# Output projection of the first pass in float16 pairs, both halves' weights resident, and the mLSTM half of blocks 3 to 8 behind the first attention

## The chip, the cores and the metric

The kernel runs on one core of a Trainium2 chip. The time is the device time of one execution in microseconds (us), as the median of several runs. TensorE multiplies matrices, VectorE and ScalarE work on vectors and on functions of them, GpSimd is a third, slower vector engine, and SyncE issues DMAs. In the profile they are PE (with PEld for weight loads), DVE, ACT, POOL and SP. Each engine takes its instructions in a fixed order that is laid down when the kernel is built.

## What is computed

One layer of a hybrid backbone: attention and an mLSTM side by side on one input projection, one output projection for both, then a SwiGLU feed-forward. There are 128 prompt tokens and 1024 latent tokens, so nine blocks of 128 tokens.

```python
D_MODEL = 1024; N_Q_HEADS = 8; HEAD_DIM = 64; MLSTM_HEADS = 4; D_FF = 2816

def trunk_layer(x, mods, ..., w_out, norm2_w, w_gu, w_down, rope, ctx_kv, init_f, init_b):
    h = rmsnorm(x, norm1_w) * (1 + sc1) + sh1
    aq, ak, av, mq, mk, mv, mo, mg = jnp.split(h @ w_in, SPLIT_POINTS, axis=-1)
    ...                                            # rmsnorm and axial rotary on aq, ak
    attn_o = attention(aq, keys, vals)             # latent tokens see 128 cached + 1024 keys
    hm, st_f, st_b = mlstm_bidir(...)              # both directions, chunks of 128
    hm = rmsnorm(hm, mlstm_norm_w) * jax.nn.sigmoid(mo)
    mix = jnp.concatenate([attn_o, hm], axis=-1) @ w_out      # (tokens, 1024) @ (1024, 1024)
    x = x + g1 * mix
    h2 = rmsnorm(x, norm2_w) * (1 + sc2) + sh2
    x = x + g2 * swiglu(h2, w_gu, w_down)
```

## The kernel before

**Passes.** The nine blocks are worked in three passes of three blocks (CB = 3) through attention, output projection, norm2 and feed-forward. Pass 0 has the prompt (block 0) and latent blocks 1 and 2, pass 1 blocks 3 to 5, pass 2 blocks 6 to 8. Before pass 0 come the input projections, the mLSTM scan of all blocks (its result goes to `hm_d` in device memory) and the first query projections.

**Number formats.** A float32 product is made of three products of a high and a low part. The input projection uses float16 pairs with a power-of-two scale (lines 487 to 489). The output projection and the feed-forward use pairs in a rounded float32 (`F32R`, in the profile f32 or fp32r): a weight block of 128x1024 is loaded as `raw`, ScalarE casts it to `whi` (line 151), and VectorE or GpSimd subtracts to get `wlo` (line 134).

**Attention** (`attention`). Blocks 1 and 2 have eight heads each; I number the 16 heads 0 to 15. A head is six score matmuls into `S` (line 1075), the row maximum on VectorE (1077), the exponential on ScalarE (1078), two small VectorE steps, the scaled high half `ph` on ScalarE (1081), the low half `pl` on VectorE (1082), and two DMA transposes (1083, 1084). `S` has one buffer. Two heads later the values product `po` follows (18 matmuls, line 999), then `ol` on ScalarE and `oT` on VectorE (1001, 1003). The next query blocks (`QREST`, in three groups) are projected beside the first heads by `weave`, 24 steps of projection to 9 of attention; their rotary runs on GpSimd (lines 639 to 657) with tables in the pool `qp`.

**Output projection of pass 0.** `w_out` has two halves of 512 rows: the attention's and the mLSTM's. `prefill` makes the mLSTM half of all nine blocks beside the attention: per block a row of `hm_d` is loaded and transposed (line 113) into `aTh`/`aTl`, then 24 matmuls of 512 columns (`out_block`, lines 1184 to 1186) are added to x, for blocks 0 to 5 in the resident `x1`, for blocks 6 to 8 through buffers `t2` (a ring of three): load x (1233), product (1235), sum on GpSimd (1236), store to `x1_d` (1237). `attn_out` then makes the attention half of blocks 0 to 2 as their heads finish, and norm2 of each: `stats` (a square on ScalarE, `rsqrt` with some ten small VectorE steps), `y` on ScalarE (1297), eight transposes, `fl`, `aTh` and `aTl`. Behind it `gate_up_pair` makes the gate/up products of the first two blocks of 128 columns of the feed-forward for 256 of the 384 tokens, and the main feed-forward starts with the other 128 tokens of them.

**What sets the order.** The generators yield pieces, and loops such as `weave` draw from several of them; the engines' orders come out of that and of a list scheduler with priorities (`hot`). The first attention draws one piece of `prefill` and `attn_out` for each of its own; behind it, the next attention is drawn 0.3 to 1 while the rest of `attn_out` runs. Buffers from pools are reused, so a tile of a new pool waits for the last user of the memory below it.

## Time and profile before

| | |
|---|---|
| median of 3 runs | 1619.37 us (1618.15 to 1621.2) |
| profiled execution | 1617.88 us, its span 1616.1 us |
| TensorE busy | 1521.3 us, 94% |
| VectorE, ScalarE, GpSimd busy | 940.1, 730.2, 615.8 us |
| mean granted TensorE clock | 0.968 |
| instructions | 23209 |

How to read it: a span is the time between the first and the last instruction. A row of instructions reads: start, duration, engine, line of the kernel, operation, output <- inputs, shape, count, and in brackets the idle time of the engine ahead of it with what ended it. A row of a group has count, busy time and mean duration, then idle time with its releasers. A matmul's duration overlaps that of its neighbours. The granted clock is a share of full speed.

### The profile page before, as it was taken

Reading aid. Unit: us, or ns where it says so; the run is one execution under the profiler, and the core shown is the slowest. Engines: PE = TensorE matmul, PEld = TensorE weight load, DVE = VectorE, ACT = ScalarE, POOL = GpSimd, SP = SyncE. Lnnn points to the kernel's source line nnn. Section 1 sums busy time; section 2 is a strip of 40 time slices with the busy share of each in tenths; the row PEclk is TensorE's granted clock in tenths of the full one; section 3 lists DMA queues with packets and bytes.
Section 4 is the critical chain, followed back from the end, with each engine's and each line's share of the span. In section 5 each row is a group of like instructions: output and inputs, shape, how many; then the busy total and the mean of one; then the engine's idle time right before and its main releaser. Section 6 shows DMA issues by size and latency. Waiting matters only on the chain. (4 is left out here: it accounts for less than half of the span.)

```text
span 1616.1 us, 23209 instructions
## 1 busy us (share of the span) xinstructions
PE 1521.3 (94%) x8688; PEld 1260.8 (78%) x8688; DVE 940.1 (58%) x1821; ACT 730.2 (45%) x1240; POOL 615.8 (38%) x376
## 2 busy tenths in 40 slices
PE   5899999899788868999999999999999999999996
PEld 2655665576557758988999999898898989999995
DVE  3944353947787565677753547767764474332445
ACT  3744343435454455655532344565552443333322
POOL 0411020503247453433345344443344445544443
PEclk8899999999899987999999999999999999999998
DMA  9445353211165664787843546787774445534441
GB/s 344 132 131 144 102 134 73 84 19 32 41 171 119 147 159 100 166 194 169 190 146 118 156 144 208 189 180 165 169 178 124 142 134 174 156 122 147 143 130 66
DMA packets 383270, 227.98 MB, mean 141 GB/s; under 512 B 169174, under 2 KB 345766, under 8 KB 383158
## 3 DMA queue, kind: packets, MB, share of 16 engines
q1 hardware_dynamic: 382598, 225.68, 52.9%
q8 instruction: 68, 1.11, 0.3%
q10 hardware_dynamic: 560, 0.83, 0.1%
q14 instruction: 44, 0.36, 0.1%
HBM read 178.80 MB, written 9.33 MB: 116 GB/s over the span
## 5 line engine op out<-in xcount | busy, mean ns | idle before, releaser
L134 POOL TENSOR_TENSOR wlo<-raw,whi 128x1024 fp32r<-128x1024 f32 x146 | 357.8, 2454 | 450.3 <-ACT whi L151 416.4
L151 ACT CAST whi<-raw 128x1024 fp32r<-128x1024 f32 x219 | 224.3, 1025 | 372.0 <-DMA raw<-in_w_gu_dram 127.8
L1334 PE MATMUL mm<-aTl,whi 128*128 128x384 f32 (+2 forms) x1088 | 366.8, 337 | 0.0
L1335 PE MATMUL mm<-aTh,wlo 128*128 128x384 f32 (+2 forms) x1088 | 366.4, 337 | 0.0
L1333 PE MATMUL mm<-aTh,whi 128*128 128x384 f32 (+2 forms) x1088 | 365.1, 337 | 0.9 <-DVE tn L1361 0.9
L1333 PEld LDWEIGHTS mm<-aTh,whi 128*128 128x128 f32 x1088 | 206.9, 190 | 2.1 <-DVE tn L1361 1.5
L1334 PEld LDWEIGHTS mm<-aTl,whi 128*128 128x128 f32 x1088 | 206.9, 190 | 1.0 <-POOL aTl L134 0.3
L1335 PEld LDWEIGHTS mm<-aTh,wlo 128*128 128x128 f32 x1088 | 207.0, 190 | 0.1
L134 DVE TENSOR_TENSOR wlo<-raw,whi 128x1024 fp32r<-128x1024 f32 (+1 forms) x73 | 88.2, 1208 | 132.9 <-ACT whi L151 132.7
L1152 PE MATMUL mm<-whi,hl 128*128 128x512 f32 x372 | 147.0, 398 | 1.0 <-ACT hl L1365 0.9
L1153 PE MATMUL mm<-wlo,hl 128*128 128x512 f32 x372 | 147.2, 397 | 0.0
L1154 PE MATMUL mm<-whi,hl 128*128 128x512 f32 x372 | 144.4, 397 | 0.7 <-POOL hl L134 0.7
L1082 DVE SCALAR_TENSOR_TENSOR pl<-pr,st,ph 128x1152 f16<-128x1152 f32 x64 | 109.5, 1711 | 46.7 <-ACT ph L1081 46.6
L487 PE MATMUL wi<-ipair,hT 128*128 128x384 f16 (+2 forms) x384 | 124.9, 326 | 2.8 <-ACT ipair L215 2.8
L488 PE MATMUL wi<-ipair,hT 128*128 128x384 f16 (+2 forms) x384 | 124.9, 325 | 0.0
L489 PE MATMUL wi<-ipair,hT 128*128 128x384 f16 (+2 forms) x384 | 124.4, 325 | 0.3 <-POOL hT L134 0.3
L1361 DVE SCALAR_TENSOR_TENSOR tn<-tn,mm 128x384 f32<-128x384 f32 (+2 forms) x68 | 36.7, 540 | 144.4 <-PE mm L1335 110.0
L134 POOL TENSOR_TENSOR hl<-tn,hl 128x384 fp32r<-128x384 f32 x66 | 81.9, 1241 | 96.5 <-ACT hl L1365 90.4
L1142 DVE TENSOR_TENSOR x<-x,t 128x512 f32<-128x512 f32 x102 | 116.1, 1158 | 0.8
L1078 ACT ACTIVATE pr<-S,st 128x1152 f32<-128x1152 f32 x64 | 78.3, 1223 | 80.4 <-DVE st L1077 77.6
L1141 DVE TENSOR_TENSOR t<-mm,gl 128x512 f32<-128x512 f32 x106 | 70.8, 683 | 40.6 <-PE mm L1154 15.8
L1077 DVE TENSOR_REDUCE st<-S 128x1 f32<-128x1152 f32 x64 | 86.5, 1351 | 13.2 <-PE S L1075 12.8
(370 smaller groups left out, 2678.0 us busy)
## 6 DMA issues: line engine op xcount, KB each, us to landing
raw<-in_w_gu_dram SPq DMA_DIRECT2D x132, 512.0 KB
raw<-in_w_down_dram SPq DMA_DIRECT2D x60, 512.0 KB
a<-in_w_ada_dram SPq DMA_DIRECT2D x32, 512.0 KB
gl<-g_d SPq DMA_DIRECT2D x36, 256.0 KB
aw<-in_w_ada_dram SPq DMA_DIRECT2D x16, 512.0 KB
iraw<-in_w_in_dram SPq DMA_DIRECT2D x32, 256.0 KB
raw<-in_w_out_dram SPq DMA_DIRECT2D x15, 512.0 KB
x<-in_x_sample_dram SPq DMA_DIRECT2D x13, 512.0 KB
```

Of the source, the lines that this page charges most:

```text
L134: (dve if eng == "dve" else pool).tensor_tensor(out=out, in0=full, in1=hi, op=ALU.subtract)
L151: nc.scalar.copy(hi[:, :n], raw[:, :n])
L487: mm(ps[:, :n], ah, wh[:, k % 2, c0 : c0 + n], start=(k == 0), stop=False)
L488: mm(ps[:, :n], ah, wl[:, k % 2, c0 : c0 + n], start=False, stop=False)
L489: mm(ps[:, :n], al, wh[:, k % 2, c0 : c0 + n], start=False, stop=(k == KD - 1))
L1142: eng.tensor_tensor(out=x1[:, cs], in0=x1[:, cs], in1=t, op=ALU.add)
L1152: mm(ps, ah, wh[:, k % 2, :], start=(k == 0), stop=False)
L1153: mm(ps, ah, wl[:, k % 2, :], start=False, stop=False)
L1154: mm(ps, al, wh[:, k % 2, :], start=False, stop=(k == nk - 1))
L1333: mm(ps, wh[:, k, :], th[:, k, :], start=(k == 0), stop=False)
L1334: mm(ps, wh[:, k, :], tl[:, k, :], start=False, stop=False)
L1335: mm(ps, wl[:, k, :], th[:, k, :], start=False, stop=(k == KD - 1))
```

## The change

`out_scale` reads all of `w_out` once, early, for one power-of-two scale; the mLSTM half's four blocks stay resident. `out_pairs` makes float16 pairs of them: `hpair` in the pool `xp`, whose memory lies over that of `qp`, and `apair` for the attention half, which is loaded a second time. The left-hand sides become float16 pairs too (`halves16`), and the products are scaled back as they are added (`add_scaled`). `prefill` is now one generator for each block, and `attn_first` takes the place of `attn_out` in pass 0. `first_rows` sets the order: blocks 0 and 1 of the mLSTM half, then attention block 0, then one more mLSTM block, attention block 1, and the other mLSTM blocks behind the first attention, beside attention block 2. The next attention is no longer drawn in this part. The scaling of v goes from VectorE to ScalarE; `weave` is 24 to 10.

ScalarE around heads 8 and 9 (`pr` is the exponential, `ph` the high half, `S` the scores). Before:

```order
L1078 ACTIVATE pr_5416,st_5419<-S_5420,st_5419 128x1152
L1001 ACTIVATE ol_5499<-po_5480,vsc 64x256
L1081 ACTIVATE ph_5417<-pr_5416,st_5419 128x1152
L1220 CAST aTh_5254<-mm_5875 128x4x128
L151 CAST xhi<-xraw 128x1024
L1078 ACTIVATE pr_5451,st_5454<-S_5455,st_5454 128x1152
L1081 ACTIVATE ph_5452<-pr_5451,st_5454 128x1152
```

After, from head 8's exponential to head 9's second step, with the four weight pairs between them:

```order
L1127 ACTIVATE pr_5479,st_5482<-S_5483,st_5482 128x1152
L1130 ACTIVATE ph_5480<-pr_5479,st_5482 128x1152
L974 ACTIVATE hpair_5308<-oraw_4452,osc 128x1024
L978 CAST hpair_5311<-oraw_4454 128x1024
L974 ACTIVATE hpair_5315<-oraw_4456,osc 128x1024
L978 CAST hpair_5318<-oraw_4458 128x1024
L1127 ACTIVATE pr_5514,st_5517<-S_5518,st_5517 128x1152
L1050 ACTIVATE ol_5555<-po_5536 64x256
L1243 ACTIVATE lhs_5458<-mm_5451,hms 128x512
L1240 CAST lhs_5533<-oT_4879 128x512
L1130 ACTIVATE ph_5515<-pr_5514,st_5517 128x1152
```

The pairs were `whi` casts ahead of head 4 before; now they stand between two heads. TensorE, before, at head 3, where the projection matmuls of the mLSTM half stand around its scores:

```order
L1186 MATMUL mm_5349<-whi_5269,aTl_5255 128x512
L1075 MATMUL S_5018<-kst_4226,qT_4739 128x384 x6
L999 LDWEIGHTS vs
L999 MATMUL po_4956<-phT_4766,vs 128x256
L999 LDWEIGHTS vs
L999 MATMUL po_4956<-plT_4767,vs 128x256
L1184 MATMUL mm_5349<-whi_5275,aTh_5254 128x512
L1184 MATMUL mm_5398<-whi_5257,aTh_5254 128x512
```

After, at heads 5 to 7 (the three `S` rows), where only values stand between scores:

```order
L1048 MATMUL po_5232<-plT_5024,vs 128x256
L1124 MATMUL S_5205<-kst_4235,qT_4793 128x384 x6
L1124 MATMUL S_5350<-kst_4235,qT_4793 128x384 x6
L1048 LDWEIGHTS vs
L1048 MATMUL po_5411<-phT_5168,vs 128x256
L1124 MATMUL S_5380<-kst_4235,qT_4793 128x384 x6
L1048 LDWEIGHTS vs
L1048 MATMUL po_5411<-plT_5169,vs 128x256
```

The first projection matmul of the change stands behind head 9's scores. ScalarE after, at head 11 (its exponential is the last row but one here; `jk` to `fl` are norm2 of block 0):

```order
L1330 ACTIVATE jk_5613,s_1107_5612<-x_1040_5294 128x1024
L1346 ACTIVATE y_5634<-x_1040_5294,ry_5616 128x512
L1346 ACTIVATE y_5666<-x_1040_5294,ry_5616 128x512
L1354 ACTIVATE fl_5633<-mm_5636,shift_76,scale_75 128x128 x3
L1127 ACTIVATE pr_5647,st_5650<-S_5651,st_5650 128x1152
L1354 ACTIVATE fl_5633<-mm_5668,shift_76,scale_75 128x128 x3
```

Norm2 of block 0 moved from behind the attention to the middle of it. TensorE after, at the end of the first attention: the last values (18 matmuls, the last of them here) and the first matmuls of mLSTM block 3 (`lhs_5987`) and attention block 2 (`lhs_5976`):

```order
L1048 MATMUL po_5953<-plT_5829,vs 128x256
L1232 LDWEIGHTS lhs_5987
L1232 MATMUL mm_5990<-hpair_5308,lhs_5987 128x512
L1233 LDWEIGHTS lhs_5987
L1233 MATMUL mm_5990<-hpair_5308,lhs_5987 128x512
L1232 LDWEIGHTS lhs_5976
L1232 MATMUL mm_6006<-apair_5330,lhs_5976 128x512
```

Blocks 3 to 8 of the mLSTM half stand behind the last values now, where the scores of the next attention were. The diff, cut to its core:

```diff
+    def out_load(half):
+        raws = []
+        for n in range(2):
+            for j in range(2):
+                r0 = half * 512 + 2 * j * P
+                raw = wp.tile([P, 1024], F32, name=nm("oraw"), tag="wlo", bufs=5)
+                dma(raw..., w_out[r0 : r0 + 2 * P, n * 512 : (n + 1) * 512]...)
+                raws.append(raw)
+        return raws
+
+    def out_scale(kept):
+        for half in range(2):
+            raws = out_load(half)
+            for _ in range(4):
+                yield
+            for j, raw in enumerate(raws):
+                jk = wp.tile([P, 1024], BF16, name=nm("jk"), tag="raw", bufs=2)
+                act(jk, raw, AF.Abs, accum_out=osc[:, 4 * half + j : 4 * half + j + 1])
+                yield
+        kept.extend(raws)
+        dve.tensor_reduce(out=osc[:, 8:9], in_=osc[:, 0:8], axis=AX.X, op=ALU.max)
+        yield from power_scale(gp, one1, osc[:, 8:9], osc[:, 9:11])
...
+    def out_pairs(raws, new):
+        ws = [[], []]
+        for j, raw in enumerate(raws):
+            w = new(j)
+            hi, lo = w[:, 0], w[:, 1]
+            if j % 2 == 0:
+                act(hi, raw, AF.Copy, scale=osc[:, 9:10])
+                dve.scalar_tensor_tensor(out=lo, in0=raw, scalar=osc[:, 9:10], in1=hi, op0=ALU.mult, op1=ALU.subtract)
+            else:
+                act(raw, raw, AF.Copy, scale=osc[:, 9:10])
+                nc.scalar.copy(hi, raw)
+                sub(lo, raw, hi, "pool")
+            ws[j // 2].append(...)
+        return ws
...
-    weave(linear_tok(w_q, 0, 512, ev_q, QFIRST), beside((scan, 3.0), (key_stacks(), 0.2)), 16, 16)
+    weave(linear_tok(w_q, 0, 512, ev_q, QFIRST), beside((scan, 3.0), (key_stacks(), 0.2), (oscale, 1.2)), 16, 16)
...
-        dve.tensor_scalar(out=v, in0=v, scalar1=vsc[:, 0:1], scalar2=None, op0=ALU.mult)
-        dve.tensor_copy(vs[:, i0 : i0 + 5, :, 0], v)
+        act(v, v, AF.Copy, scale=vsc[:, 0:1])
+        nc.scalar.copy(vs[:, i0 : i0 + 5, :, 0], v)
...
-    weave(linear_tok(w_q, 0, 512, ev_q, QREST, bank), att, 24, 9)
+    weave(linear_tok(w_q, 0, 512, ev_q, QREST, bank), att, 24, 10)
...
+    def halves16(src, scale):
+        t = wp.tile([P, 2, 4, P], F16, name=nm("lhs"), tag="wlo", bufs=5)
+        if scale is None:
+            nc.scalar.copy(t[:, 0], src)
+            sub(t[:, 1], src, t[:, 0], "dve")
+        else:
+            act(t[:, 0], src, AF.Copy, scale=scale)
+            dve.scalar_tensor_tensor(out=t[:, 1], in0=src, scalar=scale, in1=t[:, 0], op0=ALU.mult, op1=ALU.subtract)
+        return t[:, 0], t[:, 1]
+
+    def add_scaled(x, ps, inv, g):
+        t = t2()
+        dve.scalar_tensor_tensor(out=t, in0=ps, scalar=inv, in1=g, op0=ALU.mult, op1=ALU.mult)
+        pool.tensor_tensor(out=x, in0=x, in1=t, op=ALU.add)
...
+    def attn_first(i, a, o, ws, gs, gx, ahead=None):
+        x1 = a["x1"][i]
+        with hot(500):
+            th, tl = halves16(o, None)
+        yield
+        for n in range(2):
+            cs = slice(n * 512, (n + 1) * 512)
+            ps = out_block(ws, n, th, tl)
+            with hot(200):
+                add_scaled(x1[:, cs], ps, osc[:, 12:13], gx[n] if i == 0 else gs[n])
+            yield
+        with hot(200):
+            a["rs"] += stats([x1])
+        if ahead is not None:
+            yield from ahead
+        yield from norm2(0, a, i)
...
+    hm_ws = out_pairs(hm_raws, lambda j: xp.tile([P, 2, 1024], F16, name=f"hpair{j}"))
+    at_ws = out_pairs(out_load(0), lambda j: wp.tile([P, 2, 1024], F16, name=nm("apair"), tag="whi", bufs=5))
+    cur["rs"] = []
+    fill = chain(*[prefill(b, (cur["x1"], nxt["x1"]), hm_ws, gs, gx) for b in range(NB)])
+
+    def first_rows():
+        for _ in range(6):
+            next(fill)
+            yield
+        for i in range(CB - 1):
+            while i not in done:
+                next(fill, None)
+                yield
+            yield from attn_first(i, cur, oT[i], at_ws, gs, gx)
+            for _ in range(3 if i == 0 else 0):
+                next(fill)
+                yield
...
     for _ in att:
-        due += 1.0
+        due += 1.3
...
+    for _ in chain(side, attn_first(CB - 1, cur, oT[CB - 1], at_ws, gs, gx, gate_up_pair(cur, range(2)))):
+        for _ in range(2):
+            next(fill, None)
+    emit(fill)
     oT = []
     att = attention(1, oT, set())
-    due = 0.0
-    for i, _ in enumerate(side):
-        if i >= 6:
-            due += 0.3
-            while due >= 1.0:
-                next(att)
-                due -= 1.0
```

More of the change, by code (lines that the diff above doesn't have):

```diff
@@ L707, in hybrid_step @@
     dve.tensor_scalar(out=mwh, in0=mwh, scalar1=0.5, scalar2=None, op0=ALU.mult)
+    dve.tensor_reduce(out=hms[:, 0:1], in_=mwh, axis=AX.X, op=ALU.max, apply_absolute_value=True)
+    dve.tensor_scalar(out=hms[:, 0:1], in0=hms[:, 0:1], scalar1=2.0 * P ** 0.5, scalar2=None, op0=ALU.mult)
+    powers(hms, P)
     def qcol(i, d, b, h):
@@ L962, in hybrid_step @@
     emit(scan)
+    emit(oscale)
     es1.close()
@@ L1158, in three_blocks, with out_pieces @@
                 done(i, ps)
-    def out_pieces(half, own=None):
+    def out_pieces(half):
         ws = []
@@ L1166, in out_pieces @@
                 rows = w_out[r0 : r0 + 2 * P, n * 512 : (n + 1) * 512].rearrange("(a p) n -> p a n", p=P)
-                pieces.append(load_piece([(full_view, rows)], (2, 512), raw=own and own[2], own=own))
-                own = None
+                pieces.append(load_piece([(full_view, rows)], (2, 512)))
             ws.append(pieces)
@@ L1240, in attn_out @@
-    def attn_out(c, a, oT, gs, gx=None, ready=None, then=None, ahead=None):
+    def halves16(src, scale):
[7 more added lines that the diff above has]
+        return t[:, 0], t[:, 1]
@@ new lines, in add_scaled, with load_hm, prefill @@
+    def add_scaled(x, ps, inv, g):
+        t = t2()
+        dve.scalar_tensor_tensor(out=t, in0=ps, scalar=inv, in1=g, op0=ALU.mult, op1=ALU.mult)
+        pool.tensor_tensor(out=x, in0=x, in1=t, op=ALU.add)
+    hm_rows = {}
+    def load_hm(b):
+        if b < NB:
+            hm_rows[b] = t2()
+            dma(hm_rows[b], hm_d[b * P : (b + 1) * P, :])
+    def prefill(b, x1s, ws, gs, gx):
+        c, i = divmod(b, CB)
+        if b + 1 < 2 * CB:
+            dma(x1s[(b + 1) // CB][(b + 1) % CB], xrow(b + 1))
+        hm = hm_rows.pop(b)
+        ps = bank()
+        for j in range(4):
+            transpose(ps[:, j * P : (j + 1) * P], hm[:, j * P : (j + 1) * P])
+        load_hm(b + 1)
+        th, tl = halves16(ps.rearrange("p (j x) -> p j x", j=4), hms[:, 2:3])
+        yield
+        for n in range(2):
+            cs = slice(n * 512, (n + 1) * 512)
+            ps = out_block(ws, n, th, tl)
+            g = gx[n] if b == 0 else gs[n]
+            if c < 2:
+                add_scaled(x1s[c][i][:, cs], ps, osc[:, 11:12], g)
+            else:
+                xt = t2()
+                dma(xt, xrow(b)[:, cs])
+                add_scaled(xt, ps, osc[:, 11:12], g)
+                dma(x1_d[i][:, cs], xt)
+            yield
@@ new lines, in attn_first @@
+    def attn_first(i, a, o, ws, gs, gx, ahead=None):
[3 more added lines that the diff above has]
+        yield
+        for n in range(2):
+            cs = slice(n * 512, (n + 1) * 512)
+            ps = out_block(ws, n, th, tl)
+            with hot(200):
[6 more added lines that the diff above has]
+        yield from norm2(0, a, i)
@@ L1242, in attn_out @@
+    def attn_out(c, a, oT, gs):
         ws = None
         x1 = a["x1"]
-        a["rs"] = []
         for i in range(CB):
-            while ready is not None and i not in ready:
-                yield False
-            b = c * CB + i
-            if gx is None and i != 1:
+            if i != 1:
                 t = ap.tile([P, NQ, P], F32R, name=nm("mx"), tag="qT", bufs=2)
@@ L1256, in attn_out @@
                 nc.scalar.copy(th, o)
-                sub(tl, o, th.bitcast(F32), "dve" if gx is None else "pool")
-            if then is not None and i > 0:
-                yield from then(i - 1)
+                sub(tl, o, th.bitcast(F32), "dve")
             yield True
-            ws = ws or out_pieces(0, spare if gx is not None else None)
+            ws = ws or out_pieces(0)
             for n in range(2):
@@ L1264, in attn_out @@
                 with hot(200):
-                    add_gated(x1[i], ps, gx[n] if b == 0 else gs[n], n, pool if gx is not None else dve)
+                    add_gated(x1[i], ps, gs[n], n)
                 yield True
-            if then is not None:
-                with hot(200):
-                    a["rs"] += stats(x1[i : i + 1])
-        if then is not None:
-            yield from ahead
-            yield from then(CB - 1)
-        else:
-            with hot(200):
-                a["rs"] = stats(x1)
+        with hot(200):
+            a["rs"] = stats(x1)
     def stats(rows):
```

72 lines of the change are left out of this document (17 added, 55 removed).

## The prediction

> **What bounds the kernel now.** I read the page first (busy shares, the slices, the granted clock), then a table by stretches of the time around the change, then the groups of TensorE instructions in it, then its waits. From the page:
>
> ```profile
> span 1616.1 us, 23209 instructions
> PE 1521.3 (94%) x8688; PEld 1260.8 (78%) x8688; DVE 940.1 (58%) x1821; ACT 730.2 (45%) x1240; POOL 615.8 (38%) x376
> ...
> PE   5899999899788868999999999999999999999996
> ...
> PEclk8899999999899987999999999999999999999998
> ```
>
> TensorE is the bound nearly everywhere. A slice is 40.4 us; the slices below 9 between 400 and 650 us are the first attention and the first output projection, where the change works. After 650 us TensorE has no room: work pushed there costs its full length. So I count what TensorE could have done in the stretch and did not. I take it from the first projection matmul (473.7) to the last matmul of the early gate/up (658.5), in three parts: until the ninth head's row maximum, until the last attention output, and the rest.
>
> ```profile
> 473.70:533.10 59.40, 53.60 (x276) 44.01 (x276) 46.18 (x85) 27.61 (x37) 40.62 (x27) 0.94 0.59 139
> 533.10:599.90 66.80, 56.97 (x270) 45.26 (x268) 43.44 (x69) 35.29 (x50) 31.31 (x18) 0.87 0.77 178
> 599.90:658.50 58.60, 48.33 (x310) 45.16 (x308) 30.14 (x62) 32.41 (x52) 19.11 (x12) 0.83 0.43 94
> ...
> L1185 PE MATMUL mm<-wlo,aTh 128*128 128x512 f32 x72 | 29.7, 413 | 0.0
> ...
> L1075 PE MATMUL S<-kst,qT 128*128 128x384 f32 x120 | 28.1, 373 | 5.3 <-ACT pr L1078 5.2
> L999 PE MATMUL po<-phT,vs 128*128 128x256 f16 x91 | 25.2, 302 | 4.0 <-DVE st L1077 2.3 <-DMA phT<-ph 1.7
> ...
> L1335 PE MATMUL mm<-aTh,wlo 128*128 128x128 f32 x32 | 10.4, 326 | 0.0
> ...
> L1333 PE MATMUL mm<-aTh,whi 128*128 128x256 f32 x32 | 9.4, 294 | 0.0
> ```
>
> Columns of the first three: stretch and length, then busy time and count for TensorE, weight loads, VectorE, ScalarE, GpSimd, then the granted clock. The mean duration overlaps its neighbours, so a matmul's price is the distance between starts:
>
> ```profile
> 437.00 0.63 PE L487 MATMUL mm<-ipair,hT 128*128 128x512 f16 x1
> 437.42 0.63 PE L488 MATMUL mm<-ipair,hT 128*128 128x512 f16 x1
> ...
> 440.18 0.38 PE L489 MATMUL mm<-ipair,hT 128*128 128x512 f16 x1
> 440.40 0.38 PE L487 MATMUL mm<-ipair,hT 128*128 128x512 f16 x1
> ...
> 520.04 0.39 PE L1186 MATMUL mm<-whi,aTl 128*128 128x512 f32 x1
> 520.27 0.40 PE L1184 MATMUL mm<-whi,aTh 128*128 128x512 f32 x1
> ...
> 480.05 1.21 PE L1075 MATMUL S<-kst,qT 128*128 128x384 f32 x6
> 481.10 0.28 PE L999 MATMUL po<-phT,vs 128*128 128x256 f16 x1
> ...
> 596.83 0.27 PE L999 MATMUL po<-plT,vs 128*128 128x256 f16 x1
> 596.94 0.27 PE L999 MATMUL po<-phT,vs 128*128 128x256 f16 x1
> ```
>
> Prices: float16 512 columns 0.216 us, float32r 512 columns 0.233, six score matmuls 1.05, a value matmul 0.11, and the first two rows are float16 matmuls at half clock, 0.43. The stretch holds 288 projection matmuls (67 us), 20 heads' scores (21), 182 values (20), some 60 transposes (priced like values, 6.6), 96 gate/up matmuls of 256 columns and 96 of 128 (three lines of 32 each; priced like values, which have 256 columns: 21) and ten of the next group (1.7): 137.5 us of work in 184.8. So 47 us are lost now, to idle time and to the half clock behind it.
>
> **The change, part by part.**
>
> *Float16.* 288 matmuls at 0.216 instead of 0.233: -4.9 us of TensorE. It is inside the counts below.
>
> *Scale of w_out.* Four loads run one after another through one slot, and four ScalarE reductions on them stand in ScalarE's order ahead of the scan's exponentials.
>
> ```profile
> 333.73 0.63 ACT L818 ACTIVATE dt<-mm,QT 128x128 f32<-128x128 f32 x2 [16.44 <-PE mm L815]
> ...
> 433.93 0.69 PE L1025 MATMUL S<-kst,qT 128*128 128x128 f32 x2 [4.39 <-DVE qT L134]
> ```
>
> ScalarE idles 16.4 us here, and that idle time covers most of the loads; if the cover fails, the exponentials come late and TensorE waits: 0 to 6 us, I take 1, because the cover is the longest idle time in the place. Later ScalarE scales the projection's attention weights ahead of the casts that the first attention waits for (the third row), behind another load: 0 to 5 us, I take 2 (one block's load is covered by the block before it, which leaves two ScalarE passes like an exponential, 1.22). The four reloaded 512 KB blocks are covered by the query projection, on which TensorE works without a gap from 434. So is the scaling of v, which goes from VectorE to ScalarE (without that cover some 1 us, two passes); the constant factor on the attention output costs nothing.
>
> *Heads 3 to 9 without projection work.* The float16 weight pairs of the mLSTM half lie where the rotary tables lie until GpSimd's third rotary group ends. In ScalarE's order the pairs stand behind head 8; on TensorE no projection matmul stands ahead of head 9. In the kernel before, the first one runs right behind head 2. When does the third group end?
>
> ```profile
> 485.79 1.91 POOL L639 TENSOR_TENSOR qk<-qk,ry 128x1024 f32<-128x1024 f32 x1 [2.28 <-DVE ry L130]
> ...
> 499.79 3.52 POOL L657 TENSOR_TENSOR qk<-qk,nr 128x1024 f32<-128x1024 f32 x1
> ...
> 513.54 1.91 POOL L639 TENSOR_TENSOR qk<-qk,ry 128x1024 f32<-128x1024 f32 x1 [5.34 <-issue]
> ...
> 526.61 2.37 POOL L657 TENSOR_TENSOR qk<-qk,nr 128x1024 f32<-128x1024 f32 x1
> ...
> 574.65 1.34 DVE L1077 TENSOR_REDUCE st<-S 128x1 f32<-128x1152 f32 x1
> 579.96 1.36 DVE L1077 TENSOR_REDUCE st<-S 128x1 f32<-128x1152 f32 x1 [0.90 <-PE S L1075]
> ...
> L1078 ACT ACTIVATE pr<-S,st 128x1152 f32<-128x1152 f32 x64 | 78.3, 1223 | 80.4 <-DVE st L1077 77.6
> ...
> L1082 DVE SCALAR_TENSOR_TENSOR pl<-pr,st,ph 128x1152 f16<-128x1152 f32 x64 | 109.5, 1711 | 46.7 <-ACT ph L1081 46.6
> ```
>
> Now it ends at 529.0. A group alone is about 11 us (the second took 17.5 with projection additions among its steps, which the change takes out of this place); between two groups lie a ScalarE square and VectorE steps, 10.2 us now, some 9 with nothing else on VectorE. So 485 + 11 + 9 + 11 = 516. The scaled first pair follows about 1.2 us later, and the first projection matmul comes near 518. From 473.7 that is 44.3 us with seven heads' scores (7.4) and four pairs of heads' values (7.9): 29 us lost, against 9.7 of 59.4 now (work there: 136 projections 31.7, scores 7.4, values 8.1, transposes 2.6). Bounds: a head's chain of maximum, exponential and scores is 1.35 + 1.22 + 1.05 us, and 5.3 with its gaps, as the last two maxima stand; six heads at that rate would be ready at 506, if GpSimd were; with GpSimd as now, 529.
>
> *Heads 10 to 15.* TensorE's order here, each step priced as above: block 0 ends near 525 (its last pair needs three ScalarE steps and a 2.4 us GpSimd subtraction), block 1 and head 11 until 533.3, attention block 0 until 538.5. Then the transposes of norm2 for block 0 stand next in TensorE's order, and nothing behind them can run; ScalarE holds head 11's exponential behind the same chain. That wait is on record for another block:
>
> ```profile
> 599.83 0.40 PE L1186 MATMUL mm<-whi,kst 128*128 128x512 f32 x1
> 607.56 0.69 PE L113 MATMUL mm<-ident,y 128*128 128x128 f32 x2 [7.34 <-ACT y L1297]
> ...
> PE mm L113 <- ACT y L1297: 11.2, 3, 7.3
> PE po L999 <- DMA plT<-pl: 5.4, 4, 2.1
> ...
> L1084 SPq DMA_TRANSPOSE plT<-pl x13: 1241/1299/2427, 501.1 to 596.5; - x13
> ```
>
> With 7.3 us it ends at 546; head 12's scores follow at 550, 48 projection matmuls (10.4) until 561, heads 13 to 15 chained until the last exponential near 574.5. Then come its two halves (1.3 and 1.7), the DMA transpose (1.3 to issue, and up to 2.1 that TensorE waited for it), values (2), and the casts of attention block 2 (3.1 in four steps), which on ScalarE stand ahead of the left-hand side of block 3: 586. That is 68 us with 45 of work (120 projections 25.9, scores 6.3, five pairs 9.8, transposes 3): 23 lost.
>
> *The rest as filler.* 168 projection matmuls (36.3), early gate/up (21.1) and transposes (2.7): 60.1 us, dense, and it covers the last norm2 chain, which had little cover before (its share of the 11.2 us waited). But blocks 6 to 8 go through a ring of three buffers (load, product, store), and 6 halves took:
>
> ```profile
> 542.03 0.68 DVE L1235 TENSOR_TENSOR t<-mm,gl 128x512 f32<-128x512 f32 x1
> ...
> 570.39 0.69 DVE L1235 TENSOR_TENSOR t<-mm,gl 128x512 f32<-128x512 f32 x1
> ```
>
> 28.4 us from first to last, hidden under heads. TensorE now reaches them in about 22 us, with four banks of slack: 0 to 8 us, I take 2.5. The w_gu loads stand behind the last stores on SyncE's queue; two blocks loaded ahead hide that. And each of the two stalls above leaves the clock halved for one burst, as the float16 rows show it behind the wait at 433.93 (some 6 us at half rate, 3 lost): 0 to 6, I take 3.4, since both bursts are short of that one. So the main feed-forward starts at 586 + 60.1 + 5.9 = 652.
>
> *What is still owed then.* At 658.5 the kernel before had done seven heads of the next attention (7.4), two pairs' values (3.9), query transposes (0.9) and ten matmuls of the next group (1.7): 13.9 us, now in the stretch that is TensorE-bound. 652 + 13.9 = 665.9, against 658.5: +7.4. Earlier steps +3. Sum **+10.4**. The profiled execution took 1617.88 us (1.5 below the median of the runs, 1619.37): 1617.9 + 10.4 = **1628**.
>
> [...]
>
> **Rivals.** *Pairs ready early (faster).* If GpSimd ends the third rotary group by about 503, the pairs are converted as head 8 ends, heads 9 to 15 move up by some 14 us, and the dense tail starts at 572: 1628 - 14 = 1614, and 1610 if half of the norm2 wait is covered too (two of the three such waits now share 3.9 of 11.2). It wins from a first projection matmul before about 506 (12 us ahead of mine). For it: the last two heads now stand 5.3 us apart. Against: the rotary chain, where each group waits for the one before.
>
> *GpSimd no earlier than now (much slower).* VectorE's second half of a softmax lies on GpSimd's steps:
>
> ```profile
> 498.54 2.51 DVE L1082 SCALAR_TENSOR_TENSOR pl<-pr,st,ph 128x1152 f16<-128x1152 f32 x1
> ```
>
> It took 2.51 instead of its mean of 1.71, while the rotary step beside it took 3.52 instead of 2.37. With heads closer together this happens more often; a third group at 526 gives 1628 + 10 = 1638. [...]
>
> *No change.* The lost time is the same in another place: my three parts lose 29 + 23 + 5.9 = 58 us, and with float16's 4.9 some 50 would be even. A norm2 wait that is covered (7.3) and no early delay (3) do that: 1618.
>
> **How the numbers follow.** A measurement here tells 0.2% (3.2 us) from no change. Forecast, slower by 4 to 16 us: 0.45. GpSimd late: 0.15, 1633 to 1645. Pairs early: 0.30, 1604 to 1615. No change: 0.10. So faster 0.30, same 0.10, slower 0.60; the range 1608 to 1641 leaves out the far ends of the first two rivals. The forecast's own range is 1622 to 1634, from the bounds of the ring, the clock and the early delays.
>
> **What would show it.** Right: TensorE busy below half between 480 and 515, half the clock there; the first hpair cast between 512 and 522, with GpSimd as its releaser; an idle time of 5 us or more before norm2's transposes after the first attention block; 8 us or more idle or sparse after head 15; no head of the next attention before the main feed-forward. Wrong: the first hpair matmul before 506, or the last attention value before 575, or no idle time before block 3.

## The result, and the profile after

The changed kernel takes 1666.34 us (1657.66 to 1666.69, four runs) against 1618.76 us for the kernel before beside it: ratio 1.0299 (1.0273 to 1.0326), **48 us slower**. The forecast was 10 us slower, and the range ended at 1641. The direction was right, the size was not.

The page of the changed kernel:

```profile
span 1664.9 us, 23245 instructions
...
PE 1534.9 (92%) x8691; PEld 1247.5 (75%) x8691; DVE 936.4 (56%) x1836; ACT 743.7 (45%) x1264; POOL 606.6 (36%) x372
...
PE   5899998889876869999999999999999999999996
...
PEclk8999999999886879999999999999999999999999
```

A slice is 41.6 us. TensorE's digit is lower than before in the seventh and the ninth slice (250 to 291 us, which is ahead of the change, and 333 to 375), and it is lowest in the twelfth to fifteenth (458 to 624), with the clock low in the same slices. The same three stretches as in the prediction (533.1 is the row maximum of head 9, the tenth), and the piece up to the start of the main feed-forward (columns: stretch and length, then busy time and count for TensorE, weight loads, VectorE, ScalarE, GpSimd, then clock and DMA):

```profile
473.70:533.10 59.40, 34.53 (x149) 24.26 (x148) 43.50 (x72) 33.76 (x43) 33.46 (x20) 0.67 0.58 132
533.10:599.90 66.80, 48.95 (x238) 30.04 (x236) 41.64 (x78) 31.34 (x51) 22.01 (x15) 0.86 0.36 75
599.90:658.50 58.60, 50.09 (x267) 30.01 (x268) 19.49 (x36) 13.38 (x21) 21.19 (x14) 0.89 0.30 84
658.50:678.30 19.80, 19.46 (x141) 15.11 (x140) 5.93 (x8) 4.68 (x9) 11.04 (x8) 1.00 0.57 172
```

Before, the first of these held 53.6 us of TensorE work at clock 0.94; now it holds 34.5 at 0.67. As far as that goes, this is what the prediction said. Where the delay grows, by places that both traces have:

| place | before | forecast | after | delay forecast | delay measured |
|---|---|---|---|---|---|
| a matmul ahead of the change's first instruction | 307.1 | - | 310.1 | 0 | +3.0 |
| first row maximum | 451.9 | 454.9 | 462.3 | +3 | +10.4 |
| first matmul on an mLSTM pair | - | 521 | 532.9 | - | - |
| block 3's first projection matmul | - | 589 | 608.9 | - | - |
| start of the main feed-forward (384 columns) | 658.5 | 655 | 678.3 | -3.5 | +19.8 |
| 896th of its matmuls (owed attention done) | 940.3 | - | 975.4 | +10.4 | +35.1 |
| its last matmul | 1586.2 | - | 1635.0 | +10.4 | +48.8 |

(The forecast's 518, 586 and 652 are shown with its 3 us of early delay.) So of the 38 us of surprise 7 arise before the first row maximum, 16 between there and the main feed-forward, and 15 behind its start, nearly all after 975, where the prediction expected no difference at all. The 3.0 us of the first row are not the change's: its first instruction, a load, comes at 317.0.

### The profile page after: what moved, and what is told of

Its sections match the earlier page's. It is cut to its first block, busy times and chain, and to the rows that moved or that the text cites. A ratio compares the mean times of both kernels' runs of the same rounds, so it can differ in the third digit from the quotient of the medians.

```text
span 1664.9 us, 23245 instructions
## 1 busy us (share of the span) xinstructions
PE 1534.9 (92%) x8691; PEld 1247.5 (75%) x8691; DVE 936.4 (56%) x1836; ACT 743.7 (45%) x1264; POOL 606.6 (36%) x372
## 5 line engine op out<-in xcount | busy, mean ns | idle before, releaser
L134 POOL TENSOR_TENSOR wlo<-raw,whi 128x1024 fp32r<-128x1024 f32 (+1 forms) x142 | 345.2, 2432 | 480.2 <-ACT whi L151 469.6
L151 ACT CAST whi<-raw 128x1024 fp32r<-128x1024 f32 (+1 forms) x212 | 217.0, 1024 | 365.6 <-DMA raw<-in_w_gu_dram 149.3
L1191 DVE TENSOR_TENSOR x<-x,t 128x512 f32<-128x512 f32 x102 | 110.8, 1102 | 0.9
L1048 PEld LDWEIGHTS <-vs 128*128 128x128 f16 x584 | 58.3, 106 | 58.5 <-issue 28.5
L1048 PE MATMUL po<-phT,vs 128*128 128x256 f16 x292 | 78.4, 300 | 25.0 <-DMA phT<-ph 16.4
```

Of the source, the lines that this page charges most:

```text
L134: (dve if eng == "dve" else pool).tensor_tensor(out=out, in0=full, in1=hi, op=ALU.subtract)
L151: nc.scalar.copy(hi[:, :n], raw[:, :n])
L1048: mm(po[:, 0:256], v, rhs(t, n), start=(n == 0 and t == 0), stop=(n == nk - 1 and t == 1))
```

## The experiments

Ratios are to the kernel before, run in turn with each on the same chip, since its own median moved between 1612.75 and 1618.80 us from one group of runs to the next. 0.01 is 16.2 us. Places are read from one profiled execution each, and these drift apart before the change begins: the matmul that the kernel before starts at 307.1 us comes 3.0 us later in the changed kernel, 4.6 earlier in e3, 4.7 earlier in e5, 6.4 earlier in e8, 1.1 earlier in e9, 0.9 later in e10, and 5.0 earlier in e11, which has the instructions of the kernel before. Where a place is said to be counted from 307, this offset is taken off.

| run | what it is | ratio | interval |
|---|---|---|---|
| - | the change | 1.0299 | 1.0273 to 1.0326 |
| e1 | change, weight buffers 128 bytes further than before | 1.0289 | 1.0251 to 1.0327 |
| e2 | before, weight buffers 96 bytes further | 1.0040 | 1.0020 to 1.0061 |
| e3 | change, constant scale | 1.0195 | 1.0160 to 1.0230 |
| e4 | change, norm2 of block 0 later | 1.0279 | 1.0249 to 1.0309 |
| e5 | change, mLSTM pairs early | 1.0159 | 1.0131 to 1.0187 |
| e6 | change, next attention drawn in the tail | 1.0306 | 1.0276 to 1.0335 |
| e7 | e3 with the old addresses | 1.0164 | 1.0128 to 1.0201 |
| e8 | e3, e4, e5, e6 and e7 together | 1.0107 | 1.0074 to 1.0140 |
| e9 | float16 pairs and the scaling of v on ScalarE, old order | **0.9919** | 0.9892 to 0.9947 |
| e10 | e9 with the measured scale | 1.0040 | 1.0021 to 1.0060 |
| e11 | before, 64 bytes further | 1.0019 | 0.9996 to 1.0043 |
| e12 | before, 128 bytes further | 1.0034 | 1.0017 to 1.0052 |
| e13 | e9 with blocks 3 to 8 moved | 1.0067 | 1.0046 to 1.0088 |
| e14 | e9 with late pairs | 1.0090 | 1.0059 to 1.0121 |
| e15 | e10's loads without its reductions, constant scale | 0.9956 | 0.9936 to 0.9977 |
| e16 | e10 with three buffers for the loads | 0.9977 | 0.9959 to 0.9996 |

Where a scale is constant, it is 2 to the power 15, which holds for these weights; the change measures it from w_out.

### Measuring the scale (e3, e10, e15, e16)

In the changed kernel, ScalarE's timeline around the scan (start, duration, and in brackets the idle time before and what ended it):

```profile
320.73 1.06 ACT L959 ACTIVATE jk<-oraw 128x1024 bf16<-128x1024 f32 x1 [0.38 <-DMA oraw<-in_w_out_dram]
...
334.65 1.06 ACT L959 ACTIVATE jk<-oraw 128x1024 bf16<-128x1024 f32 x1 [12.78 <-DMA oraw<-in_w_out_dram]
...
339.67 1.06 ACT L959 ACTIVATE jk<-oraw 128x1024 bf16<-128x1024 f32 x1 [3.87 <-DMA oraw<-in_w_out_dram]
...
344.69 1.06 ACT L959 ACTIVATE jk<-oraw 128x1024 bf16<-128x1024 f32 x1 [3.87 <-DMA oraw<-in_w_out_dram]
...
345.75 0.61 ACT L823 ACTIVATE dt<-mm,QT 128x128 f32<-128x128 f32 x2
...
346.87 1.23 PE L849 MATMUL mm<-va,sd 128*128 128x129 f32 x4 [6.35 <-DVE sd L825]
```

Four buffers of the ring hold query weights that still wait for their own scale, so the loads of w_out go one by one through the fifth: load, reduce, load. The scan's exponentials, at 333.7 before, stand behind in ScalarE's order and come at 345.8, 9 us later counted from 307, and TensorE then waits 6.35 us.

**e3**, the change without measuring:

```
-            for j, raw in enumerate(raws): act(jk, raw, AF.Abs, accum_out=osc[...])
...
-        yield from power_scale(gp, one1, osc[:, 8:9], osc[:, 9:11])
+        kept.extend(out_load(1))
+        dve.memset(osc[:, 9:10], 2.0 ** 15)
+        dve.memset(osc[:, 10:11], 2.0 ** -15)
```

> The changed kernel with the scale of w_out written as the constant 2^15 (the value that the measurement gives) instead of measured: four of the eight early loads, the eight ScalarE reductions and the step that spreads the scale are left out. Theory (early delay): the first scan's exponentials no longer stand behind serial loads on ScalarE, head 0's row maximum comes at 452 to 455 instead of 462.3, the first weight pair 8 to 10 us earlier than 527.2, and the time is 1656 to 1659. Rival (absorbed): the pairs wait for GpSimd's rotary groups anyway and start near 525, and the time is 1663 to 1667.

Measured 1651.16 us, ratio 1.0195: the measuring costs 15 to 17 us (against e1 and the change). That is more than the theory gave, and the rival falls. First row maximum 443.0 instead of 462.3; 7.6 of these 19.3 us are there at 307, so the measuring delays it by some 12.

**e10** puts the measuring onto e9 (below), with the scalars in the table vsc:

```
-    vsc = cp.tile([P, 8], F32, name="vsc")
+    vsc = cp.tile([P, 24], F32, name="vsc")
+    osc = vsc[:, 8:22]
... (out_scale as in the change)
```

> The ninth run with the scale of w_out measured as the change does, its scalars in the same table (weight buffers 64 bytes further). Theory (the measuring delays the scan and the first scores by some 10 us, which nothing gives back): 10 to 15 us slower than the ninth run, ratio 1.000 to 1.008. Rival (the heads' order of before hides the delay): within 4 us of the ninth run.

1.0040 against 0.9919: 20 us, more than the theory's 10 to 15; some 3 of them (0 to 7 by e11's interval, below) can be the 64 bytes. Nothing gives the delay back: the first row maximum is 14.2 us later than in e9, the last gate/up matmul 18.4 (12 and 16 counted from 307).

**e15** tells apart whether the traffic or ScalarE's order costs this: the loads remain, nobody reduces them.

```
+        for half in range(2):
+            raws = out_load(half)
+            for _ in range(8): yield
+        kept.extend(raws)
```

> The ninth run (constant scale) with the loads of the measuring (all of w_out) but without its ScalarE reductions. If the loads' traffic costs the 17 us: ratio 1.000 or more, as the tenth run. If ScalarE's order does (a reduction waits for its load, the scan's exponentials wait behind it): within 4 us of the ninth run, ratio 0.990 to 0.995, the scan's first exponential of this place at 332 to 336.

0.9956, 6 us above e9 and 14 below e10: between the two expectations, nearer to ScalarE's order. ScalarE's timeline of e15:

```profile
334.73 0.63 ACT L822 ACTIVATE dt<-mm,QT 128x128 f32<-128x128 f32 x2 [16.45 <-PE mm L819]
...
395.92 1.06 ACT L970 ACTIVATE oraw<-oraw 128x1024 f32<-128x1024 f32 x1 [11.48 <-DMA oraw<-in_w_out_dram]
```

The scan's exponentials are back at their old place, with the 16.45 us of idle time that the prediction counted on. A later operation, the scaling of a reloaded block, now waits 11.48 us for its load in the same manner, and its first row maximum is at 452.4 instead of 443.7 (2 of these 8.7 us are there at 307); I read the 6 us from that row, but no run takes that wait away alone.

**e16** mends e10: the first four loads go through the two buffers of the tag raw, where they are reduced in place, and only the second four through the one slot; that makes three buffers.

```
-            raws = out_load(half)
+            raws = out_load(half, "wlo", 5) if half else out_load(half, "raw", 2)
```

> The tenth run (old order, measured scale) with the first four loads spread over three buffers instead of one, reduced in place. If the wait is one slot's round trip, load after load: the scan's exponential comes 8 to 10 us earlier than in the tenth run (344), and 5 to 10 us are won, ratio 0.998 to 1.001. If the loads are slow by themselves: as the tenth run, 1.004.

0.9977, 10 us below e10; the scan's exponentials are at 338.6 (5.1 earlier, less than forecast), since ScalarE still waits long for the third load that it reduces:

```profile
335.36 1.06 ACT L959 ACTIVATE oraw<-oraw 128x1024 f32<-128x1024 f32 x1 [11.45 <-DMA oraw<-in_w_out_dram]
...
338.63 1.12 ACT L823 ACTIVATE dt<-mm,QT 128x128 f32<-128x128 f32 x4
```

In ScalarE's order two more passes over w_out and then the exponentials stand behind the one that waited 11.45 us for its load, and they start only after it, at 336.54, 337.60 and 338.63.

### The addresses (e1, e2, e7, e11, e12)

The change's two small tables, osc and hms, take 96 bytes per partition ahead of the weight buffers. Three TensorE timelines, each with the first and the last of the same 168 gate/up matmuls without another between them (kernel before, changed kernel, e12):

```profile
1455.05 0.34 PE L1333 MATMUL mm<-aTh,whi 128*128 128x384 f32 x1
...
1484.00 0.34 PE L1335 MATMUL mm<-aTh,wlo 128*128 128x384 f32 x1
```

```profile
1502.33 0.34 PE L1382 MATMUL mm<-aTh,whi 128*128 128x384 f32 x1
...
1531.72 0.34 PE L1384 MATMUL mm<-aTh,wlo 128*128 128x384 f32 x1
```

```profile
1458.50 0.34 PE L1333 MATMUL mm<-aTh,whi 128*128 128x384 f32 x1
...
1488.01 0.34 PE L1335 MATMUL mm<-aTh,wlo 128*128 128x384 f32 x1
```

Over 167 steps: 0.1733 us before, 0.1760 after, 0.1767 in e12, for the same duration of 0.34 in the record. The kernel has 3072 such matmuls: 2.6 ns each is 8 us.

**e1** widens hms so that the buffers lie at multiples of 64 again, 128 bytes from their old place.

```
-    hms = cp.tile([P, 4], F32, name="hms")
+    hms = cp.tile([P, 12], F32, name="hms")
```

> The changed kernel with its small table hms widened from 4 to 12 columns, which moves every weight buffer by 32 bytes, back to a multiple of 64; nothing else. Theory (address): the 384-column gate/up matmuls start 0.1759 us apart in the changed kernel and 0.1734 before because the two new tables (96 bytes) push the weight buffers to 32 modulo 64; the spacing returns to 0.1734, and 3072 of them give back about 8 us: 1658. Rival (run): the spacing belongs to the execution, not to the address: it stays near 0.176 and the time near 1666.

1664.45 us: nothing won, the distance is 0.1767. That theory fell. But the 512-column matmuls of the down projection became faster, 0.2276 instead of 0.2331 (means over a trace).

**e2** moves only the addresses of the kernel before, by the change's 96 bytes.

```
-    vsc = cp.tile([P, 4], F32, name="vsc")
+    vsc = cp.tile([P, 32], F32, name="vsc")
```

> The kernel before with its table vsc widened from 4 to 32 columns, unused: every weight buffer moves by 96 bytes, as the change moves them; nothing else. Theory (address): gate/up spacing 0.176 instead of 0.1734 and about 8 us slower, 1627. Rival (run): no difference, 1619.

0.1760 and ratio 1.0040: the address alone does it, and it costs 6.5 us of time (3 to 10 by the interval).

**e7** is e3 with its scalars inside vsc, so that all buffers lie where they lay.

```
-    vsc = cp.tile([P, 4], F32, name="vsc")
-    osc = cp.tile([P, 14], F32, name="osc")
-    hms = cp.tile([P, 4], F32, name="hms")
+    vsc = cp.tile([P, 8], F32, name="vsc")
+    hms = vsc[:, 4:8]
... (the constant 2 to the power 15 stands in the instructions)
```

> The constant scale of the third experiment, with its few scalars put into an existing table, so that every weight buffer has the address that it has in the kernel before. Theory (the 96 bytes cost the gate/up matmuls 2.4 ns each): distance between 384-column float32r matmuls back to 0.1736 us, end 6 to 8 us below the third experiment's 1651.2, near 1644. Rival (the distance comes from what else runs beside it, DMAs and VectorE at other times): distance stays near 0.1759, end within 3 us of 1651.

0.1733, ratio 1.0164 against 1.0195. The intervals overlap; in the two traces the eleventh matmul of the main feed-forward starts at 659.2 and 659.5 (e3), and the last one comes 6.6 us earlier in e7.

**e11 and e12** are the kernel before with vsc 24 and 40 columns wide (64 and 128 bytes).

```
-    vsc = cp.tile([P, 4], F32, name="vsc")
+    vsc = cp.tile([P, 24], F32, name="vsc")      (e12: 40)
```

> The kernel before with weight buffers 64 bytes further up (the table vsc 24 columns wide instead of 4), nothing else. If only a shift by an odd multiple of 32 hurts: distance of 384-column matmuls 0.1736, no change. If any distance from the old address hurts: 0.175 to 0.177, 4 to 8 us slower.

> The kernel before with weight buffers 128 bytes further up. The first run (the change, 128 bytes) had 0.1766 for 384 columns and 0.2278 for 512. If the address alone sets both: the same here, some 9 us more on gate/up and 5 us less on the down projection, so 2 to 6 us slower than before. If it was something of the change: 0.1736 and 0.2321, no change.

64 bytes: 0.1733, and 1.0019 (0.9996 to 1.0043), no change that can be told. 128 bytes: 0.1767 and 0.2277, as in e1, and 1.0034: the address sets both. No simple rule (64 bytes, any shift) fits the four values.

### Order and pairs (e4, e5, e6, e8, e9, e13, e14)

**Why the pairs are so late.** The changed kernel's timelines from the end of GpSimd's third rotary group:

```profile
522.15 2.34 POOL L659 TENSOR_TENSOR qk<-qk,nr 128x1024 f32<-128x1024 f32 x1
...
527.21 1.13 ACT L974 ACTIVATE hpair<-oraw,osc 128x1024 f16<-128x1024 f32 x1
...
529.35 5.32 POOL L134 TENSOR_TENSOR hpair<-oraw,hpair 128x1024 f16<-128x1024 f32 x2 [4.86 <-ACT hpair L978]
...
529.53 6.22 DVE L975 SCALAR_TENSOR_TENSOR hpair<-oraw,osc,hpair 128x1024 f16<-128x1024 f32 x2
...
532.87 1.06 PE L1232 MATMUL mm<-hpair,lhs 128*128 128x512 f16 x2
```

The group ends at 524.5, which is 62.2 us behind the first row maximum (the prediction had 64.1). But then 8.4 us pass instead of 2: ScalarE has head 8 ahead of the cast, and the lower halves take 3.1 us each on VectorE, beside GpSimd's; the same operation on an attention pair, at 480.2, took 1.28, with GpSimd idle. No run takes GpSimd's part away alone, so what made the difference is open.

**e5** exchanges the memories of the pairs, and also puts the remaining mLSTM work ahead of the early gate/up.

```
-    hm_ws = out_pairs(hm_raws, lambda j: xp.tile(..., name=f"hpair{j}"))
-    at_ws = out_pairs(out_load(0), lambda j: wp.tile(..., name=nm("apair"), tag="whi", bufs=5))
+    hm_ws = out_pairs(hm_raws, lambda j: wp.tile(..., name=nm("hpair"), tag="whi", bufs=5))
+    at_ws = out_pairs(out_load(0), lambda j: xp.tile(..., name=f"apair{j}"))
... (and all remaining mLSTM work ahead of the early gate/up)
```

> The change with the memories of the two weight pairs exchanged: the mLSTM half's pairs lie where the query weights lay (free early), the attention half's pairs where the rotary tables lie; all of the remaining mLSTM work stands ahead of the early gate/up. Theory (heads 3 to 9 ran bare because the pairs waited for the rotary groups): first projection matmul on an mLSTM pair near 475 instead of 533, TensorE above 80% busy between 480 and 520, the main feed-forward 18 to 25 us earlier (near 656), end near 1643 (1636 to 1650). Rival (given back: with projection work among them the heads come as late as in the kernel before, and the ends of the mLSTM blocks load VectorE and GpSimd): the ninth row maximum moves from 522 to 530 or later, and the end gains under 8 us, 1658 or more.

1637.63 us, 1.0159: 23 us won, by both edits together. First such matmul 479.0, main feed-forward 655.1 instead of 678.3; counted from 307 that is 15.5 us earlier, and the last gate/up matmul 22. TensorE is 78% busy between 480 and 520, where the theory had over 80. The theory holds in place and nearly in size; from the first row maximum to the ninth (head 8) the heads take 62.2 us instead of 59.6, a little of what the rival said. The kernel is still 26 us slower than before.

**e4** puts norm2 of block 0 behind one more mLSTM block.

```
-            yield from attn_first(i, cur, oT[i], at_ws, gs, gx)
-            for _ in range(3 if i == 0 else 0): next(fill); yield
+            yield from attn_first(i, cur, oT[i], at_ws, gs, gx, three() if i == 0 else None)
```

> The changed kernel with norm2 of block 0 behind one more block of the mLSTM half, not straight behind attention block 0's products; nothing else. Theory (wait in the middle): the 19.3 us between the row maxima of heads 11 and 12 shrink to 8 to 10, the 6.5 us idle ahead of norm2's transposes is gone, and the end comes 8 to 10 us earlier, 1657. Rival (given back): the heads come earlier but TensorE waits the same time elsewhere before the dense tail, and the time is 1663 to 1667.

1.0279: 2 to 3 us, which the intervals don't tell from nothing. The changed kernel's TensorE rows, then those of e4:

```profile
560.34 1.97 PE L113 MATMUL mm<-ident,y 128*128 128x128 f32 x8 [6.50 <-ACT y L1346]
...
601.64 0.37 PE L1048 MATMUL po<-phT,vs 128*128 128x256 f16 x1 [7.79 <-DMA phT<-ph]
```

```profile
575.28 2.29 PE L1124 MATMUL S<-kst,qT 128*128 128x384 f32 x6 [4.42 <-ACT pr L1127]
...
597.07 0.37 PE L1048 MATMUL po<-phT,vs 128*128 128x256 f16 x1 [7.61 <-DMA phT<-ph]
```

The wait of 6.50 is gone, and the heads behind it wait for their exponentials instead: between the row maxima of heads 11 and 12 8.0 us pass instead of 19.3, between those of heads 12 and 13 18.1 instead of 10.7. The rival was right.

**e6** draws six more heads of the next attention in the tail, as the kernel before does.

```
+    att = attention(1, oT1, set())
     for _ in chain(side, attn_first(...)): 
         for _ in range(2): next(fill, None)
+        due += 0.3
+        while due >= 1.0: next(att); due -= 1.0
```

> The change with the next row chunk's attention drawn among the remaining mLSTM work, as the kernel before draws it (some seven heads before the main feed-forward). Theory (part of the loss is attention that starts late: it costs TensorE the same anywhere, but by being late it is not finished under the main feed-forward and the second output projection pays, 7.6 us more there): the main feed-forward starts some 14 us later than 678, and the end is 6 to 10 us earlier, near 1658. Rival (TensorE is full in both places, so that the place is nothing): end within 3 us of 1666.

1.0306: nothing that can be told. The rival was right, the place of that attention is worth nothing here.

**e8**, all of these together with e7:

> Constant scale, addresses as before, the mLSTM pairs early, norm2 of the first block behind one more mLSTM block, the next attention drawn in the tail. If the terms add: 1666.3 - 15 (scale) - 7 (addresses) - 21 (pairs) - 8 (late attention) - 2 (norm2) = 1613, range 1606 to 1622: that would be below the kernel before. Rival (the terms overlap, since an earlier stage only waits for the next one): 1625 to 1640.

1628.5 us, 1.0107. The terms overlap, as its rival said; 17 us remain. In its trace the last head is 24 us earlier than in the kernel before and the eleventh matmul of the main feed-forward 6 us later (18 and 12 counted from 307). That pointed to the tail.

**e9** therefore takes e8 with the old order: all mLSTM blocks among the heads, norm2 one block late.

```
     def first_rows():
-        for _ in range(6): next(fill); yield
+        yield from fill
-        for i in range(CB - 1):
+        for i in range(CB):
...
-        due += 1.3
+        due += 1.0
```

> Only the float16 pairs of the change: constant scale, addresses as in the kernel before, the mLSTM pairs early, and the order of the kernel before (all mLSTM blocks among the heads, norm2 one block late, the next attention drawn in the tail). Theory (what is left of the loss in the eighth run, 1.0107 of before, comes from moving blocks 3 to 8 out from under the heads: heads came 24 us earlier there, and the tail gave back 30): ratio 0.993 to 0.999, since float16 alone saves about 5 us of TensorE and heads come at before's pace; main feed-forward near 645 to 650. Rival (the float16 form itself loses, by its casts and by weights kept resident): ratio 1.005 or more.

1602.58 us, ratio **0.9919**: 13 us faster than the kernel before, more than the 4.9 us of TensorE that I had put on float16. 8 of them are there at the first row maximum (443.7 instead of 451.9; 7 counted from 307), ahead of the first projection matmul. VectorE's rows, before and then e9, show where:

```profile
430.36 2.80 DVE L970 CAST vs<-vall 128x640 f16<-128x640 f32 x2
433.19 2.63 DVE L134 TENSOR_TENSOR qT<-mm,qT 64x512 fp32r<-64x512 f32 x4
443.40 1.23 DVE L1032 TENSOR_REDUCE st<-S 128x8 f32<-128x1024 f32 x1 [7.58 <-PE S L1025]
```

```profile
427.87 2.63 DVE L134 TENSOR_TENSOR qT<-mm,qT 64x512 fp32r<-64x512 f32 x4
435.14 1.23 DVE L1072 TENSOR_REDUCE st<-S 128x8 f32<-128x1024 f32 x1 [4.64 <-PE S L1065]
```

The cast of v stood 2.80 us ahead of the step `qT` that the prompt's scores wait for. From the start of `qT` to the prompt's row maximum 10.2 us pass before and 7.3 in e9; TensorE's idle time ahead of these scores is 4.39 us before, with float16 matmuls 0.43 us apart behind it instead of 0.22 (granted clock 0.50 from 433.9 to 437.0), and 1.56 in e9. Together 5.7 us of the 13 are gained here, where nothing is in float16 pairs that wasn't before; what has changed is that v has left VectorE. No run makes that edit alone.

**e13** moves only blocks 3 to 8 out again:

```
-        yield from fill
+        for _ in range(9): next(fill); yield
...
+            (behind the last attention block: chain(fill, gate_up_pair(...)))
```

> The ninth run with one thing changed: mLSTM blocks 3 to 8 stand behind the first attention's end. Theory (under the heads they cost nearly nothing, since the heads' chain sets the pace; behind the end they cost their length): 144 projection matmuls at 0.216 are 31 us, the heads come at most 10 us earlier, so 18 to 28 us slower than the ninth run, ratio 1.003 to 1.010. Rival (the heads speed up by as much as the blocks took): within 5 us of the ninth run.

1.0067, 24 us more. The first two stretches of e9, then of e13:

```profile
473.70:533.10 59.40, 54.93 (x315) 33.73 (x313) 49.19 (x74) 31.09 (x40) 38.59 (x24) 1.00 0.58 116
533.10:599.90 66.80, 46.37 (x241) 27.61 (x240) 41.84 (x78) 36.06 (x58) 26.02 (x16) 0.87 0.57 140
```

```profile
473.70:533.10 59.40, 45.31 (x228) 28.19 (x227) 46.92 (x82) 30.72 (x41) 36.96 (x21) 0.84 0.49 98
533.10:599.90 66.80, 47.38 (x224) 28.68 (x222) 34.78 (x69) 29.03 (x49) 15.84 (x12) 0.76 0.31 60
```

In e9 all 216 mLSTM matmuls are done by the 16th row maximum, in e13 72, as in the change. The 144 others are 31 us of TensorE at 0.216. Without them the heads, from the first to the 16th row maximum, take 114.0 us instead of 120.8: 7 us back for 31 moved, which is the 24.

**e14** is e9 with the memories of the pairs as in the change (e5's edit, the other way round).

> The ninth run with one thing changed: the memories of the two weight pairs as in the change, so that the mLSTM pairs wait for GpSimd's third rotary group. TensorE's order keeps the old place of the blocks as far as the planner lets it. Theory: the first mLSTM matmul comes near 510 instead of 470, all 216 of them are then behind it, and 15 to 35 us are lost, ratio 1.002 to 1.014. Rival (heads run ahead and the blocks catch up, since TensorE has room beside the heads): under 8 us, ratio below 0.997.

1.0090, 28 us more: the first mLSTM matmul is at 518.7, and the last at 588.1 instead of 551.7.

## Why the prediction was wrong

**The ledger.** From 1.0: float16 and v on ScalarE in the old order -13 us (e9); moved blocks, late pairs and the rest of the order together +38 (e3 less the 0.0040 of e2 is 1.0155, against 0.9919; e7, which is that kernel, has 1.0164); measuring +17 (e3 to the change); addresses +6.5 (e2). The sum is 48.5, and 48 were measured; the terms are differences along one path, so that they add up by construction, and each is known to some 5 us. The moved blocks alone cost 24 and the late pairs alone 28; together less than 52, presumably because blocks that stand behind the heads anyhow don't miss the pairs under them.

By the prediction's own steps:

- *Scale of w_out, "0 to 6, I take 1", "that idle time covers most of the loads"*: this step failed. The cover was 16.4 us from 317 to 334; the four serial loads ran until 345, and the exponentials came 9 us late, counted from 307. I had seen that they share one slot, and never multiplied: four links of 5 us would be 20. One link took 13.9 us instead, and no row that I had shows such a load. By the runs, measuring cost 17 us where the sum had +3. *The load ahead of the first attention, take 2*: the wait was there, 4.2 us. Against the forecast +3, the first row maximum came 10.4 late, 7.4 counted from 307, and another term had hidden more: *the scaling of v*, taken as covered, gained some 6 us by leaving VectorE, and without measuring the row maximum is 4.4 us early (e3, counted from 307).
- *Heads 3 to 9, first matmul near 518*: 532.9. Of the 12 us that it is later than 521, 7.4 are the early delay and 4.5 the conversion of the pairs behind the rotary group; the rotary chain itself was forecast right. The first cast came at 527.2, behind ScalarE's own head 8 and not released by GpSimd. The prediction looked for half the clock between 480 and 515; that was not shown, the granted clock was 0.64 there (0.67 in the whole row from 473.7 to 533.1), between half and full.
- *Heads 10 to 15, 68 us*: 76 us, from 532.9 to 608.9. The norm2 wait was 6.5 (taken as 7.3), but the last DMA transpose held TensorE 7.8 where I had 2.1, which is most of the 8 us.
- *Filler 60.1 + 5.9*: 69.4 us, 3.4 over. *Owed attention 13.9*: 15.3 (19.8 to 35.1), of which 2.3 are the 896 matmuls' longer distance. Both about right.
- *Nothing behind 658*: this failed too, by 13.7 us. The longer distance of the other 2176 gate/up matmuls (2.6 ns each, the addresses) is 5.7 of it, a cost that the sum did not have. The rest lies around the second output projection: from the 768th to the 1152nd of them 113.3 us passed before, 121.2 after, and 118.0 even in e9. What does that was not found and not tried, so its cause stays open.

Together, in places: 7.4 + 4.5 + 8 + 3.4 = 23.3 to the start of the main feed-forward (655 forecast, 678.3), then 1.4 and 13.7: 38.4 above the forecast. 3.0 of them are the drift before 307.

**The rivals.** *Pairs ready early* had the right mechanism, though not by a faster rotary group: e5 and e9 give the pairs other memory. e5's first such matmul came at 479, and the run won 23 us; e14, which takes that memory away from e9, lost 28. e5 stayed slower than before because the other losses were left. *GpSimd late* was not it: the group ended where forecast; what was slow beside GpSimd is the conversion, 3.1 us on VectorE against 1.28. *No change* would have needed the norm2 wait covered; e4 covered it, and the wait moved to the heads behind it. The largest gap in the method: I priced the lost TensorE time place by place, and never asked what the blocks cost where they stood. Under the heads it was 7 us for 31.

**A version that beats both.** e9 (0.9919) with a constant scale; with the scale measured, as the change wants it, e16 (0.9977, interval up to 0.9996).

## What to carry to other kernels

Work beside a chain that set the pace was nearly free here; before moving such work out, ask how much faster the chain runs without it (7 us here) against its length (31 us). A reduction or a scaling that waited for its load (12.78 us in the changed kernel, 11.48 in e15) held what stood behind it on ScalarE, so count the loads' round trips through their slots and set them against the time at which the next needed instruction is due. And compare the buffers' addresses when an edit adds a small table ahead of them (96 bytes cost 6.5 us here).

## What was not expected of the hardware

The distance between float32r matmuls differed with the place of the weight buffers, with nothing else changed (e2, e11, e12): for 384 columns 0.1733 us at the old place and 64 bytes on, 0.1760 at 96, 0.1767 at 128 (in the stretches shown); for 512 columns 0.2324, 0.2333, 0.2331 and 0.2277 (means over a trace), in the order 0, 64, 96, 128. For 384 columns the values come back in other kernels at the same address: 0.1733 in e7 (the old place), 0.1760 in the changed kernel (96), 0.1767 in e1 (128). Why is open.

A load of 512 KB took from under 4 to about 12 us from its issue to the operation that waits for it. In the changed kernel the second load is issued at 324.00 and reduced at 334.65 (the wait of 12.78 above), the third is issued at 335.83 and reduced at 339.67. The slow one stands right behind four stores of the scan's state on SyncE's queue; the first row here is the last of the four:

```profile
323.47 0.43 SPq L804 DMA_DIRECT2D out_new_state_n_dram<-cs  x1
324.00 0.39 SPq L948 DMA_DIRECT2D oraw<-in_w_out_dram  x1
```

It is the same in e10 and e16, where the load behind these stores takes 10.9 and 12.4 us. Whether the stores slow it was not tried. A load that was short at one place says little of the next.
